# Two-layer trunk on one core: attention's output projection in products of 512 tokens, and a planner with another model of transfers

## The chip, the core and the metric

The kernel runs on one core of one Trainium2 chip. The metric is the device time of one execution in microseconds (us), the median of three runs; lower is better. The profiled execution is a run of its own, with its own time.

## The reference, cut to what matters

There are 1024 tokens of width 1024, fp32 throughout. Layer 0 mixes tokens with a sparse attention (an indexer scores all earlier keys, the best 256 are kept), layer 1 with a gated short convolution. Each mixer is followed by a SwiGLU network of hidden width 2816.

```python
for i in range(DEPTH):                       # DEPTH = 2
    mod = c_act @ ada_w[i] + ada_b[i]        # six vectors of 1024: shift, scale, gate, twice
    sh1, sc1, g1, sh2, sc2, g2 = [m[:, None, :] for m in jnp.split(mod, 6, axis=-1)]
    h = _rmsnorm(x, norm1_g[i]) * (1.0 + sc1) + sh1
    y = _dsa_mixer(h, ...) if i % 2 == 0 else _short_conv_mixer(h, ...)
    x = x + g1 * y
    h = _rmsnorm(x, norm2_g[i]) * (1.0 + sc2) + sh2
    x = x + g2 * _swiglu(h, w_gate, w_up, w_down)
# the end of _dsa_mixer: o is what attention gives, (1024 tokens, 1024)
    return o @ w_out                         # the product that the change is about
```

## The kernel before, in words

Every large product is made in three parts so that it keeps fp32's precision: each operand is split into a rounded half and the remainder, "hi" and "lo", and `mm3` issues hi*hi, hi*lo and lo*hi into the same PSUM bank. A weight comes from DRAM into a buffer `raw` (512 KB, two buffers) and is split by ScalarE (`whi`, a cast) and VectorE (`wlo`, a subtraction); some weights are first combined with others on VectorE (the tiles `s`).

The kernel's functions do not issue instructions in the order in which they are written. They record them in a planner, `Plan`, which then simulates the engines on the host: `cost` gives each instruction a duration, `drain` takes at each step the instruction that can start first (ties and preferences by a priority `pri`), and emits it. Each engine then runs its own list strictly in order. Because `drain` emits everything, nearly all instructions carry one line in the profile, L278. For a transfer the planner keeps one clock, `self.dma`, that advances by the bytes at a fixed rate, and takes the data as there some time after that clock. All of these transfers are issued from one queue, SyncE's (SP). Some copies (`plan.copy`) may go to ScalarE or VectorE, whichever the planner finds free sooner.

The program on TensorE runs through these stages, with times of the profiled execution: start-up (0 to 60 us), the input projection, the indexer and the selection (60 to 290), attention over eight blocks of 128 queries (290 to 591), the second half of the output projection (591 to 640), the first network (640 to about 1290), the convolution layer (about 1290 to 1580), and the second network (to 2261).

Attention's normalised output of one block of queries and one group of four heads is written by `group_end`: `tk.split` writes the hi and lo parts. Before, `attend` allocates for each pair of blocks (256 tokens) one tile `ohi` and one tile `olo` of [128, 8, 256], out of rings of three buffers. The tiles of blocks 6 and 7 so take the buffers of blocks 0 and 1.

The output projection works on halves of 512 tokens (blocks 0 to 3, blocks 4 to 7) and on eight column tiles d of 128 columns. `out_tile(half, d)` loads the weights' columns, takes a PSUM bank of 512 columns, fills its two halves of 256 columns from the two pairs (8 steps of k, three products each, so 48 products), and adds the gated result to the residual x with one VectorE instruction. Half 0 is spread over the attention blocks 4 and 5, one tile after each group of heads (380 to 492 us). Half 1 follows the last block, in `attended` (591 to 640 us); there the residual tiles are `xr` in the profile, in half 0 they are `x`.

A second kind of work is threaded through attention and later stages: the conditioning vectors. `ada_next` loads 256 KB of `ada_w` into `adaw` (two buffers) and adds it, scaled, to the sum `adacc` on VectorE. Such a step on VectorE waits for its load, and its load can only start when the step two before it has freed the buffer.

Of the kernel before, what the change touches and what calls it, by code (L numbers as in the profile page):

```python
# [10 lines left out]
F32R = mybir.dt.float32r  # L11
# [4 lines left out]
ALU = mybir.AluOpType  # L16
# [89 lines left out]

class Op:
    __slots__ = ("eng", "cost", "emit", "pri", "left", "ready", "users", "end", "stores", "lat",
                 "late", "other", "form", "table", "needs", "parked")

    def __init__(self, eng, cost, emit, pri, lat=0.0):
        self.eng, self.cost, self.emit, self.pri, self.lat = eng, cost, emit, pri, lat
# [73 lines left out]
class Plan:  # L186
# [6 lines left out]
    ROWS, COLS = (64, 128), (128, 64)  # L193
    CHANGE = {(ROWS, None): 0.285, (None, ROWS): 0.115, (None, COLS): 0.12, (COLS, None): 0.15,
              (ROWS, COLS): 0.277, (COLS, ROWS): 0.278}
    TRAIL = 1.0 / 450e3
    SPAN, SHAKE = 100, ()
    TABLES, SWITCH = (AF.Silu, AF.Sqrt, AF.Sin, AF.Exp), 1.28
    STAY = 4.0
# [37 lines left out]
    def cost(self, eng, fn, out, ins, kw):  # L237

        n = out.free
        if fn == "dma_start":  # L240
            if eng == "gpsimd":
                return 0.85, 1.6
            inside = len(ins) == 1 and all(r.store.alloc is not None for r in ins + [out])
            return {"sync": 0.65 if inside else 0.475, "scalar": 0.1}[eng], 1.6
        if eng == "tensor":
            if fn == "transpose":
                return 0.107, 0.0
            if ins[1].dtype in (F32R, BF16):
                return max(n, 64) * 17 / 38400.0, 0.0
            return max(n * 4, 512) / (4800.0 if HD in (ins[0].free, ins[0].shape[0]) else  # L250
                                      2400.0), 0.0
        psum = any(r.store.space == PSUM for r in ins + [out])
        m = max([n] + [r.free for r in ins])
        aps = sum(r.free == 1 for r in ins)
        if eng == "scalar":
            slow = {AF.Silu: 0.06, AF.Square: 0.03}.get(kw.get("func"), 0.0)
            return ((0.05 if (ins or [out])[0].store.space == PSUM else 0.095) + 0.84e-3 * n + slow +
                    (0.09 if "accum_out" in kw else 0.0) + 0.1 * aps), 0.0
        if eng == "vector":
            if fn == "memset":  # L260
                return 0.02 + 1.04e-3 * (n if n > P else 0), 0.0
            if fn in ("tensor_scalar", "tensor_copy") and not psum and "accum_out" not in kw:
                return 0.08 + (0.52e-3 if fn == "tensor_copy" else 0.59e-3) * m, 0.0
            if fn in ("tensor_tensor_scan", "reciprocal"):
                return 0.07 + (2.07e-3 if fn == "tensor_tensor_scan" else 6.25e-3) * m, 0.0
            if fn == "tensor_scalar" and "accum_out" in kw:
                return 0.14 + 1.04e-3 * m, 0.0
            return max(0.09, 0.078 + 1.04e-3 * m) + (0.05 * aps if m > 64 else 0.0), 0.0
        if fn in ("memset", "affine_select"):
            return 0.05 + 1.4e-3 * n, 0.0  # L270
        a, w = (0.28, 1.95e-3) if fn == "tensor_tensor" else (0.43, 1.3e-3)
        return a + w * (n - 1), 0.0
# [43 lines left out]
    def record(self, eng, fn, args, kw, other=None):  # L316
        vals = list(args) + list(kw.values())
        outs = [kw["out"] if "out" in kw else args[0]]
        if "accum_out" in kw:
            outs.append(kw["accum_out"])  # L320
        refs = [v for v in vals if isinstance(v, Ref)]
        ins = [v for v in refs if not any(v is o for o in outs)]
        emit = self.emitter(eng, fn, args, kw)
        shaped = outs[0] if isinstance(outs[0], Ref) else refs[0]
        func = {"func": args[2]} if fn == "activation" else {}
        cost, lat = self.cost(eng, fn, shaped, ins, {**kw, **func})
        op = Op(eng, cost, emit, self.rank(), lat)
        if "accum_out" in kw:
            op.late = 0.13 if eng == "vector" else 0.1
        if eng == "scalar" and fn == "activation":  # L330
            op.table = args[2] if args[2] in self.TABLES else None
        if other is not None:
            op.other = (other[0], self.cost(*other[:2], shaped, ins, kw)[0],
                        self.emitter(*other, args, kw))
        if fn == "dma_start":
            op.lat = lat + shaped.free * shaped.shape[0] * 4 / 380e3
        self.note(op, refs, outs)
        return op

# [157 lines left out]
    def drain(self, *pools):  # L497

        held = []
        while any(p.pending for p in pools) if pools else True:  # L500
            best, again = None, False
            for e in self.ENGINES:
# [3 lines left out]
                op = got[3][-1]  # L506
# [18 lines left out]
            t, e, heap, v = best  # L525
            op = v[-1]
# [11 lines left out]
                t = max(t, self.free[e] + self.SWITCH)  # L538
            self.free[e] = end = t + cost
            if op.lat:  # L540
                self.dma = max(self.dma, end) + (op.lat - 1.6)
                end = self.dma + 1.6 + (op.lat - 1.6) * 380e3 * self.TRAIL
                if e == "sync":
                    self.free[e] = max(self.free[e], self.dma - 2.5)
            for st in op.stores:
                if st.alloc is not None:
                    st.pool.pending -= 1
# [42 lines left out]
def blk(b):  # L590
    return slice(b * P, (b + 1) * P)
# [318 lines left out]
class Attention:  # L910
    ON_DVE, X_SECOND, X_WORK = 5, 24.5, 38.0
    T_PROJ, SLOT = 45.0, 6.2
    ON_ACT, IDX = (2, 3, 6, 7), 0.5

    def __init__(self, tk, w, w_out, ada_w, xspill):
        self.tk, self.nc, self.w, self.w_out = tk, tk.nc, w, w_out
# [419 lines left out]

    def attend(self):
        tk, nc, plan = self.tk, self.nc, self.plan
        self.o, self.banks, self.rows, tail = [], 0, 0, None
        self.steps = [(layer, j, i, k) for layer, j in ((0, 2), (0, 3), (0, 4), (0, 5), (1, 0))  # L1340
                      for i in range(NH) for k in range(KT)]
        for b in range(TB):
            if b % 2 == 0:
                self.o.append([self.op.tile([P, KT, 2 * P], F32R, name="o%s%d" % (v, b),
                                            tag="o" + v, bufs=3) for v in ("hi", "lo")])
            t0, t1 = self.t_att[b], self.t_att[b + 1]
            plan.pri = t0 - 12.0
            q = (self.at if b % 2 else self.keep).tile([P, T], F32, name="qst", tag="qst",
# [117 lines left out]
    def group_end(self, b, g, ops, sums):  # L1466
# [11 lines left out]
        flat = on.rearrange("p r t -> p (r t)")  # L1478
        plan.copy(flat, ops[:, 0:2 * P])
        nc.vector.tensor_tensor(flat, flat, bc, op=ALU.mult)  # L1480
        hi, lo = (v.part_of((b % 2, g))[:, 2 * g:2 * g + 2, blk(b % 2)] for v in self.o[b // 2])
        tk.split(on, hi, lo)

    def out_tile(self, half, d, keep=None):

        tk, nc = self.tk, self.nc
        w = tk.wcols(self.w_out, d * P, P)
        xt = self.at.tile([P, HW], F32, name="x1", tag="x1") if keep is None else keep
        nc.sync.dma_start(xt, self.xspill[half][d])
        ps = self.bank("out")  # L1490
        for i in range(2):
            ohi, olo = self.o[2 * half + i]
            for k in range(KT):
                tk.mm3(ps[:, i * 2 * P:(i + 1) * 2 * P], *w(k), ohi[:, k, :], olo[:, k, :],
                       k == 0, k == KT - 1)
        nc.vector.scalar_tensor_tensor(xt, ps, tk.mod[0][2][:, d:d + 1], xt,
                                       op0=ALU.mult, op1=ALU.add)
        if keep is None:
            nc.sync.dma_start(self.xspill[half][d], xt)

# [523 lines left out]
```

## Time and profile before

| quantity | value |
|---|---|
| median of three runs | 2261.14 us (2258.73 to 2264.98) |
| profiled execution, whole time | 2262.64 us |
| its span, first to last instruction | 2260.9 us |
| mean granted TensorE clock | 0.987 |
| TensorE busy | 2207.6 us of the span |
| VectorE busy | 1896.3 us |
| ScalarE busy | 1136.8 us |
| data moved by transfers | 353.74 MB |

PE is TensorE, PEld its weight loads, DVE VectorE, ACT ScalarE, SP SyncE (which here only issues transfers). A row of the chain of waits tells what the end of the program depended on, in order of time: start, length, what. A row of the windows view gives a stretch, its length, the busy time of PE, PEld, DVE, ACT and POOL in it with the number of instructions, the granted clock of TensorE, the share of the DMA engines and GB/s.

### The profile page before, as it was taken

The numbers are of one execution on the slowest core, as the hardware profiler recorded it, in microseconds if no ns is written. First come the engines' busy times: TensorE is split into PE (matmuls) and PEld (weight loads), VectorE is DVE, ScalarE is ACT, GpSimd is POOL, SyncE is SP. The second block draws the span as 40 slices with busy tenths as digits, with TensorE's granted clock in tenths as the row PEclk, the third lists the DMA queues.
The fourth block names the chain that finished last, engine by engine and source line by source line (L and its number), as shares of the span: only waits on it lengthen the run. The fifth ranks groups of instructions, "written<-read, shape, count | busy, mean of one in ns | idle before, by whom it ended". The sixth has DMA issues, their size and how long they took to land.

```text
span 2260.9 us, 32683 instructions
## 1 busy us (share of the span) xinstructions
PE 2207.6 (98%) x11499; PEld 1790.8 (79%) x11499; DVE 1896.3 (84%) x3819; ACT 1136.8 (50%) x2162; POOL 4.8 (0%) x19
## 2 busy tenths in 40 slices
PE   6999989999999999999999999999999999999999
PEld 5758856876888778888888787878888888888887
DVE  7899999798599989887798899886898877768974
ACT  5487999767664333333445552224553333334444
POOL 0000000000000000000000000000000000000000
PEclk7999989999999999999999999999999999999999
DMA  9413233543364656455982454234445432349824
GB/s 317 124 41 103 89 108 102 167 131 99 104 177 141 212 184 192 138 170 179 384 279 84 123 152 143 86 117 158 122 126 183 152 120 87 125 145 387 286 86 139
DMA packets 332318, 353.74 MB, mean 156 GB/s; under 512 B 19289, under 2 KB 216954, under 8 KB 332154
## 3 DMA queue, kind: packets, MB, share of 16 engines
q1 hardware_dynamic: 331944, 351.52, 48.8%
q8 instruction: 90, 1.47, 0.3%
q14 instruction: 74, 0.61, 0.1%
q10 hardware_dynamic: 210, 0.14, 0.0%
HBM read 278.97 MB, written 68.94 MB: 154 GB/s over the span
## 4 chain that ended last, share of the span: by engine, by line
PE 78%; DVE 13%; DMA 4%; issue 2%; ACT 2%; POOL 0%; ACTq 0%; SPq 0%; DVEq 0%; POOLq 0%
PE ps_g L278 44%; PE ps_mm L278 31%; DVE wlo L278 2%; PE ps_o L278 2%; DVE u L278 1%; DVE s L278 1%; PE ps_L L278 1%; DMA adaw<-in_ada_w_dram 1%; DVE sc L278 1%; DVE p L278 1%; DVE adacc L278 1%; DVE karena L278 1%; DMA raw<-in_conv_w_in_dram 1%; DMA ph<-in_ffn_w_down_dram 1%; DVE v L278 0%
## 5 line engine op out<-in xcount | busy, mean ns | idle before, releaser
L278 ACT CAST whi<-raw 128x512 fp32r<-128x512 f32 x307 | 189.4, 620 | 360.4 <-PE ps_g L278 150.0
L278 PE MATMUL ps_g<-t,whi 128*128 128x512 f32 x1184 | 366.1, 390 | 3.0 <-ACT whi L278 3.0
L278 ACT CAST whi<-s 128x512 fp32r<-128x512 f32 x276 | 171.1, 621 | 317.7 <-PE ps_g L278 133.7
L278 PE MATMUL ps_g<-h,whi 128*128 128x512 f32 x1056 | 327.6, 391 | 0.5 <-ACT whi L278 0.5
L278 DVE TENSOR_TENSOR wlo<-raw,whi 128x512 fp32r<-128x512 f32 x312 | 213.2, 687 | 74.4 <-ACT whi L278 74.0
L278 PEld LDWEIGHTS ps_g<-t,whi 128*128 128x128 f32 x1184 | 222.1, 188 | 50.1 <-ACT whi L278 4.3
L278 PE MATMUL ps_g<-t,wlo 128*128 128x512 f32 x592 | 231.1, 391 | 3.6 <-DVE wlo L278 3.4
L278 PEld LDWEIGHTS ps_g<-h,whi 128*128 128x128 f32 x1056 | 198.2, 188 | 42.1 <-ACT whi L278 1.4
L278 PE MATMUL ps_g<-h,wlo 128*128 128x512 f32 x528 | 206.3, 391 | 2.0 <-DVE wlo L278 2.0
L278 DVE TENSOR_TENSOR wlo<-s,whi 128x512 fp32r<-128x512 f32 x276 | 188.5, 686 | 18.3 <-ACT whi L278 17.7
L278 PE MATMUL ps_mm<-t,whi 128*128 128x512 f32 x608 | 189.3, 392 | 2.7 <-ACT whi L278 2.7
L278 PE MATMUL ps_g<-ph,whi 128*128 128x512 f32 x572 | 179.1, 389 | 0.0
L278 PEld LDWEIGHTS ps_mm<-t,whi 128*128 128x128 f32 x608 | 114.8, 189 | 27.9 <-ACT whi L278 3.6
L278 PEld LDWEIGHTS ps_g<-t,wlo 128*128 128x128 f32 x592 | 111.2, 188 | 29.6 <-DVE wlo L278 6.1
L278 PEld LDWEIGHTS ps_g<-ph,whi 128*128 128x128 f32 x572 | 107.3, 188 | 22.4
L278 PE MATMUL ps_mm<-t,wlo 128*128 128x512 f32 x304 | 119.7, 394 | 1.6 <-DVE wlo L278 1.6
L278 ACT ACTIVATE junk<-sc,bs 128x384 bf16<-128x384 f32 (+3 forms) x124 | 110.1, 888 | 16.0 <-DVE bs L278 9.7
L278 PEld LDWEIGHTS ps_g<-h,wlo 128*128 128x128 f32 x528 | 99.5, 189 | 23.3 <-DVE wlo L278 2.5
L278 DVE TENSOR_TENSOR u<-u 128x512 f32<-128x512 f32 x170 | 114.4, 685 | 1.9 <-ACT u L278 0.5
L278 DVE SCALAR_TENSOR_TENSOR adacc<-adaw,cact,adacc 128x512 f32<-128x512 f32 x140 | 104.4, 746 | 13.5 <-DMA adaw<-in_ada_w_dram 13.0
L278 PE MATMUL ps_g<-ph,wlo 128*128 128x512 f32 x286 | 110.3, 389 | 0.0
L278 PE MATMUL ps_mm<-ph,whi 128*128 128x512 f32 x308 | 96.6, 390 | 0.1
(328 smaller groups left out, 4792.8 us busy)
## 6 DMA issues: line engine op xcount, KB each, us to landing
adaw<-in_ada_w_dram SPq DMA_DIRECT2D x160, 256.0 KB, 3.2
ph<-in_ffn_w_down_dram SPq DMA_DIRECT2D x66, 512.0 KB, 6.7
raw<-in_ffn_w_gate_dram SPq DMA_DIRECT2D x54, 512.0 KB, 4.3
raw<-in_ffn_w_up_dram SPq DMA_DIRECT2D x54, 512.0 KB, 4.3
raw<-in_conv_w_in_dram SPq DMA_DIRECT2D x34, 512.0 KB, 5.1
raw<-in_ffn_w_down_dram SPq DMA_DIRECT2D x44, 256.0 KB, 2.6
ph<-in_ffn_w_down_dram SPq DMA_DIRECT2D x44, 256.0 KB, 4.7
raw<-in_attn_w_in_dram SPq DMA_DIRECT2D x18, 512.0 KB, 3.9
```

What stands on the lines that cost most here:

```text
L278: f(*[a.get() if isinstance(a, Ref) else a for a in args], **{k: a.get() if isinstance(a, Ref) else a for k, a in kw.items()})
```

## The change

It has two parts.

First, attention's output lies in one tile `ohi` and one `olo` of [128, 8, 3, 256], with three places for pairs of blocks; pairs 0, 1, 2, 3 take places 0, 1, 2, 1. `out_tile` issues 24 products of 512 columns for a column tile in place of 48 of 256: for half 0 from places 0 and 1, for half 1 from places 1 and 2. For half 1 the places stand in the other order than the tokens, so there the addition to the residual is made in two instructions of 256 columns.

Second, the planner's model: a product of n columns costs (n + 32) / 2400 us where it was n * 17 / 38400 (the same at 512 columns); a transfer's clock runs at 390 KB/us instead of 380, at 1.3 times the bytes where the last dimension is at most 128; the data is taken as there at the later of that clock plus 0.8 us plus a latency, and the issue plus the latency plus the bytes at 200 KB/us; the latency is 1.0 us, or 0.4 us for a transfer into DRAM, where it was 1.6. No instruction's work changes by this, only the order in which the lists are written (and which engine takes some copies).

```diff
@@ Plan: the planner's model @@
-    TRAIL = 1.0 / 450e3
+    RATE, ALONE, SHORT = 390e3, 200e3, 1.3
...
@@ cost @@
             if eng == "gpsimd":
-                return 0.85, 1.6
+                return 0.85, 1.0
             inside = len(ins) == 1 and all(r.store.alloc is not None for r in ins + [out])
-            return {"sync": 0.65 if inside else 0.475, "scalar": 0.1}[eng], 1.6
+            return {"sync": 0.65 if inside else 0.475, "scalar": 0.1}[eng], 1.0
...
             if ins[1].dtype in (F32R, BF16):
-                return max(n, 64) * 17 / 38400.0, 0.0
+                return (max(n, 64) + 32) / 2400.0, 0.0
...
@@ record @@
         if fn == "dma_start":
-            op.lat = lat + shaped.free * shaped.shape[0] * 4 / 380e3
+            op.bytes = shaped.free * shaped.shape[0] * 4 * (self.SHORT if shaped.shape[-1] <= P else 1)
+            inside = isinstance(outs[0], Ref) and outs[0].store.alloc is not None
+            op.lat = lat if inside else lat - 0.6
...
@@ drain @@
             if op.lat:
-                self.dma = max(self.dma, end) + (op.lat - 1.6)
-                end = self.dma + 1.6 + (op.lat - 1.6) * 380e3 * self.TRAIL
+                self.dma = max(self.dma, end) + op.bytes / self.RATE
                 if e == "sync":
                     self.free[e] = max(self.free[e], self.dma - 2.5)
+                end = max(self.dma + 0.8 + op.lat, end + op.lat + op.bytes / self.ALONE)
...
@@ the attention class, attend @@
+    PLACES = (0, 1, 2, 1)
...
+        self.o = [self.op.tile([P, KT, 3, 2 * P], F32R, name="o" + v) for v in ("hi", "lo")]
...
         for b in range(TB):
-            if b % 2 == 0:
-                self.o.append([self.op.tile([P, KT, 2 * P], F32R, name="o%s%d" % (v, b),
-                                            tag="o" + v, bufs=3) for v in ("hi", "lo")])
...
@@ group_end @@
-        hi, lo = (v.part_of((b % 2, g))[:, 2 * g:2 * g + 2, blk(b % 2)] for v in self.o[b // 2])
+        i = self.PLACES[b // 2]
+        hi, lo = (v.part_of((i, b % 2, g))[:, 2 * g:2 * g + 2, i, blk(b % 2)] for v in self.o)
         tk.split(on, hi, lo)
...
@@ out_tile @@
         ps = self.bank("out")
-        for i in range(2):
-            ohi, olo = self.o[2 * half + i]
-            for k in range(KT):
-                tk.mm3(ps[:, i * 2 * P:(i + 1) * 2 * P], *w(k), ohi[:, k, :], olo[:, k, :],
-                       k == 0, k == KT - 1)
-        nc.vector.scalar_tensor_tensor(xt, ps, tk.mod[0][2][:, d:d + 1], xt,
-                                       op0=ALU.mult, op1=ALU.add)
+        places = self.PLACES[2 * half:2 * half + 2]
+        i = min(places)
+        for k in range(KT):
+            keys = [(p, r, k // 2) for p in places for r in range(2)]
+            tk.mm3(ps, *w(k), *(v.part_of(keys)[:, k, i:i + 2].rearrange("p i t -> p (i t)")
+                                for v in self.o), k == 0, k == KT - 1)
+        gate = tk.mod[0][2][:, d:d + 1]
+        for c in ((0, HW),) if places[0] == i else ((2 * P, HW), (0, 2 * P)):
+            j = 0 if c[0] == 0 and c[1] == HW else 2 * P - c[0]
+            x = xt[:, j:j + c[1] - c[0]]
+            nc.vector.scalar_tensor_tensor(x, ps[:, c[0]:c[1]], gate, x, op0=ALU.mult,
+                                           op1=ALU.add)
```

The second part, with the new durations of the first, moves instructions on all engines. Three places follow; names before the arrow are written, names behind it read.

TensorE, end of attention, before: the output projection's half 1 has begun, in the gap ahead of the last products with the values, `ps_o` (`ohi_3024` and `olo_3025` belong to blocks 4 and 5; `whi` and `wlo` are weights).

```order
L278 MATMUL ps_mm<-ohi_3024,wlo 128x256
L278 MATMUL ps_mm<-ohi_3024,whi 128x256
L278 MATMUL ps_mm<-olo_3025,whi 128x256
L278 MATMUL ps_o<-pf,vst 64x128 x16
L278 MATMUL ps_mm<-ohi_3024,wlo 128x256
L278 MATMUL ps_mm<-ohi_3024,whi 128x256
L278 MATMUL ps_mm<-olo_3025,whi 128x256
```

The same place after:

```order
L278 MATMUL ps_mm<-ohi,whi 128x512
L278 MATMUL ps_mm<-olo,whi 128x512
L278 MATMUL ps_mm<-ohi,wlo 128x512
L278 MATMUL ps_o<-pf,vst 64x128 x16
L278 MATMUL ps_mm<-ohi,whi 128x512
L278 MATMUL ps_mm<-olo,whi 128x512
L278 MATMUL ps_mm<-ohi,wlo 128x512
```

Ahead of `ps_o` stand six products of 512 columns now, where eleven of 256 did; behind it the projection goes on, now with pieces of blocks 6 and 7 in every product.

VectorE, in the first network (about 789 to 800 us), before: steps of the conditioning (`adacc`), the network's gating (`u`, `v`, `cv`) and weights in preparation (`s`, `wlo`).

```order
L278 SCALAR_TENSOR_TENSOR adacc<-adaw,cact,adacc 128x512
L278 TENSOR_TENSOR wlo<-s,whi 128x512
L278 TENSOR_TENSOR u<-cv,ps_mm 128x512
L278 TENSOR_TENSOR v<-u 128x512
L278 TENSOR_TENSOR cv<-cv 128x512
L278 TENSOR_TENSOR v<-v,ps_g 128x512
L278 SCALAR_TENSOR_TENSOR adacc<-adaw,cact,adacc 128x512
L278 TENSOR_TENSOR u<-u,ps_g 128x512
L278 SCALAR_TENSOR_TENSOR adacc<-adaw,cact,adacc 128x512
L278 TENSOR_TENSOR u<-u 128x512
L278 TENSOR_TENSOR wlo<-raw,whi 128x512
L278 TENSOR_TENSOR u<-u,ps_g 128x512
```

The same place after:

```order
L278 SCALAR_TENSOR_TENSOR adacc<-adaw,cact,adacc 128x512
L278 TENSOR_TENSOR wlo<-s,whi 128x512
L278 TENSOR_TENSOR cv<-cv 128x512
L278 TENSOR_TENSOR u<-cv,ps_mm 128x512
L278 TENSOR_TENSOR v<-u 128x512
L278 SCALAR_TENSOR_TENSOR adacc<-adaw,cact,adacc 128x512
L278 TENSOR_TENSOR v<-v,ps_g 128x512
L278 TENSOR_TENSOR s<-raw 128x512 x2
L278 SCALAR_TENSOR_TENSOR adacc<-adaw,cact,adacc 128x512
L278 TENSOR_TENSOR u<-u,ps_g 128x512
L278 TENSOR_TENSOR wlo<-raw,whi 128x512
L278 TENSOR_TENSOR u<-u 128x512
```

The second `adacc` of these rows moved ahead by two instructions, and two `s<-raw` moved from behind the third `adacc` to ahead of it.

SyncE's transfers at the beginning of the convolution layer (from about 1284 us), before: weights (`raw`), conditioning (`adaw`), and a spilled tile `cv` (written to `aw`, read back later).

```order
L278 DMA adaw<-in_ada_w_dram 128x512
L278 DMA raw<-in_conv_w_in_dram 128x8x128 x2
L278 DMA adaw<-in_ada_w_dram 128x512
L278 DMA aw_0_184<-cv 128x512
L278 DMA adaw<-in_ada_w_dram 128x512
L278 DMA aw_1_185<-cv 128x512
L278 DMA raw<-in_conv_w_in_dram 128x8x128
L278 DMA adaw<-in_ada_w_dram 128x512 x2
L278 DMA aw_0_186<-cv 128x512
L278 DMA aw_1_187<-cv 128x512
L278 DMA raw<-in_conv_w_in_dram 128x8x128
```

After, the next loads of `adaw` stand further on, among the reads of the spilled tiles:

```order
L278 DMA adaw<-in_ada_w_dram 128x512
L278 DMA cv<-aw_0_184 128x512
L278 DMA raw<-in_conv_w_in_dram 128x8x128 x2
L278 DMA cv<-aw_1_185 128x512
L278 DMA adaw<-in_ada_w_dram 128x512
L278 DMA hid_0_91<-cv 128x512
L278 DMA cv<-aw_0_186 128x512
L278 DMA adaw<-in_ada_w_dram 128x512
L278 DMA cv<-aw_1_187 128x512
L278 DMA cv<-aw_0_188 128x512
L278 DMA raw<-in_conv_w_in_dram 128x8x128 x2
L278 DMA cv<-aw_1_189 128x512
```

The five loads of `adaw` that stood among the first writes of `cv` moved about 70 us of the program further, to among the reads.

More of the change, by code (lines that the diff above doesn't have):

```diff
@@ L108 @@
     __slots__ = ("eng", "cost", "emit", "pri", "left", "ready", "users", "end", "stores", "lat",
-                 "late", "other", "form", "table", "needs", "parked")
+                 "late", "other", "form", "table", "bytes", "needs", "parked")
     def __init__(self, eng, cost, emit, pri, lat=0.0):
@@ L1338, in attend @@
         tk, nc, plan = self.tk, self.nc, self.plan
-        self.o, self.banks, self.rows, tail = [], 0, 0, None
+        self.banks, self.rows, tail = 0, 0, None
+        self.o = [self.op.tile([P, KT, 3, 2 * P], F32R, name="o" + v) for v in ("hi", "lo")]
         self.steps = [(layer, j, i, k) for layer, j in ((0, 2), (0, 3), (0, 4), (0, 5), (1, 0))
```

## The prediction

> **What bounds the kernel now.** I read the page's busy times and its summary of the chain first, then the windows view cut at the stages, then the chain and the waits inside the stretches that the change touches.
>
> ```profile
> span 2260.9 us, 32683 instructions
> PE 2207.6 (98%) x11499; PEld 1790.8 (79%) x11499; DVE 1896.3 (84%) x3819; ACT 1136.8 (50%) x2162; POOL 4.8 (0%) x19
> PE 78%; DVE 13%; DMA 4%; issue 2%; ACT 2%; POOL 0%; ACTq 0%; SPq 0%; DVEq 0%; POOLq 0%
> ```
>
> PE is busy for 2207.6 of 2260.9 us and carries 78% of the chain; 53.3 us are left in which it does nothing. The windows say where those are.
>
> ```profile
> 0.00:60.00 60.00, 40.39 (x203) 35.51 (x204) 43.80 (x93) 32.73 (x57) 1.76 (x13) 0.74 0.92 321
> 290.00:380.00 90.00, 82.98 (x658) 52.82 (x656) 88.08 (x335) 88.32 (x248) 0.00 (x0) 0.92 0.34 95
> 380.00:492.00 112.00, 109.53 (x1006) 92.45 (x1005) 93.96 (x285) 80.74 (x167) 0.00 (x0) 1.00 0.49 144
> 591.00:640.00 49.00, 49.00 (x426) 48.70 (x425) 35.64 (x60) 25.61 (x43) 0.00 (x0) 1.00 0.52 164
> 640.00:780.00 140.00, 139.96 (x627) 115.72 (x626) 130.24 (x218) 65.51 (x110) 0.00 (x0) 1.00 0.59 180
> 780.00:810.00 30.00, 24.45 (x92) 18.32 (x91) 24.21 (x41) 8.66 (x15) 0.00 (x0) 0.89 0.64 201
> 810.00:1280.00 470.00, 469.45 (x2085) 387.33 (x2084) 400.62 (x651) 194.13 (x332) 0.00 (x0) 1.00 0.58 193
> 1280.00:1300.00 20.00, 17.95 (x77) 14.37 (x76) 17.85 (x35) 8.49 (x15) 0.00 (x0) 0.91 0.60 180
> 1300.00:1360.00 60.00, 60.00 (x265) 49.22 (x264) 59.94 (x101) 33.86 (x59) 0.00 (x0) 1.00 0.54 156
> 1360.00:1400.00 40.00, 36.09 (x155) 28.02 (x154) 37.96 (x68) 9.49 (x16) 0.00 (x0) 1.00 0.46 136
> 1400.00:1580.00 180.00, 177.46 (x777) 145.03 (x777) 146.02 (x247) 57.62 (x98) 0.00 (x0) 1.00 0.40 121
> ```
>
> The reader is to see three kinds of stretch. In 591 to 640 (half 1 of the output projection), 640 to 780 and 810 to 1280 PE has no gap: only less PE work makes these shorter, and another order of the other engines gains nothing there. In 290 to 380, 1300 to 1360 and 1360 to 1400 DVE (88.08 of 90, 59.94 of 60, 37.96 of 40) is about as full as PE. And in 780 to 810 and 1280 to 1300 neither is full: PE lacks 5.55 and 2.05 us and its granted clock falls to 0.89 and 0.91, worth another 0.11 x 30 = 3.3 and 0.09 x 20 = 1.8 us. An order of work can win or lose in the last two kinds and at start-up (19.6 us of idle PE beside a DMA share of 0.92).
>
> **The change, part by part. The products.** Half 1 on the chain of waits, and a run of 512-column products from the stage behind it:
>
> ```profile
> 594.60 15.55 PE ps_mm L278 x128
> 615.70 24.35 PE ps_mm L278 x203
> 657.73 2.72 PE ps_mm L278 x12
> ```
>
> A product of 256 columns follows the one before after 24.35 / 203 = 0.120 us (15.55 / 128 = 0.1215 agrees); one of 512 takes 2.72 / 12 = 0.2267 us. Two of the former become one of the latter: 0.240 - 0.2267 = 0.0133 us saved per pair. There are 8 tiles x 8 steps x 3 products x 2 pairs = 384 products in a half before and 192 after, so 192 x 0.0133 = 2.56 us a half.
>
> In half 1 the whole of it is on the path, since PE is busy 49.00 of 49.00 us: -2.56. Nothing else becomes late there: DVE has 35.64 us of work and ACT 25.61 in what will be 46.4 us. The bounds are the same row's two ends, 15.55 / 128 and 24.35 / 203: -2.56 to -2.85.
>
> In half 0 the products lie between attention's groups, in eight pieces of 48 x 0.120 = 5.76 us that become 5.44. PE is busy 109.53 of 112 us there, so it is the bound nearly throughout, but 2.47 us of waits show that DVE and ACT are close behind at some groups. All of it saved gives -2.56; none saved (each group then waits for its softmax instead) gives 0. I take -2.0, nearer to the first since PE's idle share is only 2%.
>
> One rule speaks against this price. The Trainium skill, "TensorE: Matmul & The Clock Gate", section "Back-to-back issue gap", gives an isolated product's spacing as N / 2.4 + 2.5 ns. By it a pair of 256 columns would take 218.3 ns and one of 512 takes 215.8, so all 384 pairs would save an estimated 1.0 us and not 5.1. The trace does not agree: it has 120 ns and 226.7 ns, a fixed part of about 13 ns for each product; the rows decide the sum.
>
> **The split addition.** In half 1 eight additions of 512 columns become sixteen of 256.
>
> ```profile
> L278 DVE SCALAR_TENSOR_TENSOR xr<-ps_mm,mod,xr 128x512 f32<-128x512 f32 x7 | 5.2, 748 | 0.8 <-PE ps_mm L278 0.8
> L278 DVE TENSOR_TENSOR on<-on,ps_mm 128x256 f32<-128x256 f32 x1 | 0.4, 421 | 6.4 <-ACT on L278 6.4
> ```
>
> Two of 421 ns for one of 748: 0.094 us x 8 = +0.75 us of DVE, which has 13 us to spare in the stage. What follows the last of them on PE is the first network, and 640 to 780 shows PE without a gap across that border, so the cover is the products of 512 tokens already normalised. I take 0; without the cover the last tile alone would be late, by 0.1 us, and at most by all 0.75.
>
> **The dependency that could have appeared** is that place 1 is written a second time, by blocks 6 and 7. They wait for half 0's products, as they did for the ring of three. Half 0 ends at about 492 us, and the first group of block 6 is written after that in either order: 0. At the end of attention six products of 512 (6 x 0.2267 = 1.36 us) stand ahead of the last `ps_o` where eleven of 256 (1.32 us) did, so the gap there stays filled: 0. The products behind it need blocks 6 and 7 only as far as they are done, and 18 products are free of the last group: 4.1 us, against a first visit to those blocks 3.6 us after the start (30 x 0.120) before. Bounds 0 to +1.
>
> **The new order: the conditioning in attention.** An `adacc` step waits on DVE until its load is there, and the load starts when the step two before has freed the buffer.
>
> ```profile
> DVE adacc L278 <- DMA adaw<-in_ada_w_dram: 6.8, 8, 1.2
> adaw<-in_ada_w_dram SPq DMA_DIRECT2D x160, 256.0 KB, 3.2
> ```
>
> In 380 to 492 DVE waited so 8 times, 6.8 us in all. A load takes 3.2 us from issue to landing. I counted, in the order of DVE and with the durations of the trace, the steps of attention that have less than 3.2 us of other DVE work since the buffer became free: 17 of 78 before, 22 after; the missing work sums to 10 us before and 16 after. So waits grow by 5 x (6.8 / 17) = +2.0 us on DVE, at most by the 6 us that are missing more. PE's idle time there is 2.47 us beside those 6.8, so about a third passes on: +0.7 (0 to +2.2). Behind the waiting step stand the maxima of the next group's scores, which ACT's exponentials and then PE wait for.
>
> **The stall in the first network.**
>
> ```profile
> 790.28 7.09 DMA adaw<-in_ada_w_dram
> DVE adacc L278 <- DMA adaw<-in_ada_w_dram: 3.3, 2, 2.2
> ACT whi L278 <- DVE s L278: 10.7, 5, 7.1
> 799.47 4.63 PE ps_mm L278 x10
> ```
>
> In 780 to 810 a load of `adaw` is issued at 790.28 us and lands 7.09 us later. DVE waits for it and its predecessor, 3.3 us in all; the weights `s` stand behind on DVE and ACT waits up to 7.1 us for them, and then PE. When PE starts again, ten products take 4.63 us, 0.463 each and so twice 0.2267: the clock has halved. The change moves two `s<-raw` (0.6 us each) ahead of the second wait, into time that DVE idles, so the weights behind are 1.2 us earlier; `wlo<-raw`, which PE needs first, still stands behind the same load. I take -1.2 (-4 if the load lands early enough to spare the clock's drop of 3.3 as well, +3 if one more load is caught so, the size of the 3.3 us of waits now).
>
> **The convolution layer.** Five `adaw` loads, and their steps, move from 1284 to 1300 into 1350 to 1400. There DVE has 97.9 of 100 us of work from 1300 on.
>
> ```profile
> ACT whi L278 <- DMA raw<-in_conv_w_in_dram: 14.2, 3, 5.3
> 1385.34 5.45 DMA raw<-in_conv_w_in_dram
> ```
>
> Five steps are 5 x 0.68 = 3.4 us of DVE that come out of a stretch with 2.15 us of DVE slack and go into one without, but DVE arrives there that much earlier. The loads of `raw` (one takes 5.45 us on the chain) also stand up to two places earlier in SP's queue, though they still wait for DVE to free their buffer. I take 0, between -3.9 (all of the idle PE time of 1360 to 1400) and +3.4.
>
> At start-up the weights' first loads and the transposes swap places; nothing shows which way it goes: 0, with 2 us to either side, about a tenth of its idle PE time of 19.6.
>
> **The sum.** -2.56 - 2.0 + 0 + 0.7 - 1.2 + 0 + 0 = -5.06 us, against the profiled span of 2260.9: 2255.8, and a whole time of 2262.64 - 5.06 = 2257.6. That execution stands 1.5 us above the median of 2261.14, so the median should come to 2256.1. All runs before lie between 2258.73 and 2264.98, so 0.3% (6.8 us: 2254.4 and 2267.9) is about what can be told from no change, and the forecast lies within it.
>
> **Rivals.**
> Faster, by the order: the planner's new view of transfers takes away most of what transfers cost now. For it speaks that 780 to 810, 1280 to 1300 and 1360 to 1400 hold 8.85 + 3.85 + 3.9 = 16.6 us of idle or slow PE, each with a load on the chain. Against it: in the last of these DVE is full, and in the first the same load still stands ahead. If half of it goes, 8.3 instead of my 1.2, the time is 2256.1 - 7.1 = 2249.0.
>
> Slower: the five conditioning steps in the convolution layer wait for their loads. DVE is the bound there, so each wait goes to the end in full; a load's 3.2 us five times is 16 us, and the time is 2256.1 + 16 = 2272. It would be slower than no change by over 0.3% from 11.8 us on, 2.4 us a step. For it speaks the stall at 790.28, which is this mechanism in the stage before; against it, that in attention 17 close steps cost only 6.8 us, 0.4 each. The Trainium skill, "TensorE: Matmul & The Clock Gate", section "Why this matters for your kernels", warns that a gap of TensorE over about 3 us brings half speed back; the ten products at 799.47 agree.
>
> No gain: half 0 saves nothing, because its groups wait for the softmax, and the waits for `adaw` grow by the full 2.2: -2.56 + 2.2 = -0.4, so 2260.8.
>
> **How the numbers follow.** Likeliest case 0.50, at 2256.1 with about 4 us to either side (2252 to 2260) from the terms at 780 to 810, the convolution and the start-up taken together; 0.14 of this lies below 2254.4, the rest within 0.3%. The faster rival 0.26, all but 0.01 below 2254.4. No gain 0.10, within. The slower rival 0.14, of which 0.01 ends within. Faster 0.14 + 0.25 = 0.39, same 0.36 + 0.01 + 0.10 + 0.01 = 0.48, slower 0.13. The range takes in the faster rival with 3 us below it (2246) and ends above at 2266, where the slower case has half its waits (2256.1 + 8 = 2264); what lies outside is some 0.12 above and 0.06 below.
>
> **What would show it.** Products on the chain at 0.2267 us in both halves, and half 1 about 46.4 us long with PE full; if it is still 49, the first term is wrong. In blocks 4 and 5 PE's idle time should be 2.5 to 4 us; over 5 means that half 0's saving went into waits for the softmax. The waits of `adacc` for `adaw` in attention should grow by about 2 us. Around 790 to 800 us an `adacc` should still wait, with half-speed products behind it; without them the faster rival is right. In 1360 to 1400 the list of waits should have no `adacc` over 1 us; several of 2 to 3 us are the slower rival. All stages that PE fills now should keep their length within 0.5 us. The prediction fails most easily by an order of work that leaves a stage of the second network, now without gaps, with a new one.

## The result, and the profile after

The changed kernel takes 2274.28 us (2265.66 to 2276.12, 12 runs) where the kernel before takes 2260.96 (2258.73 to 2264.98, 12 runs): a ratio of 1.0055, interval 1.0047 to 1.0062. It is 13.3 us slower; 2256.1 was forecast, and the range ended at 2266.

The page of the changed kernel, its span, its busy times and its summary of the chain:

```profile
span 2273.4 us, 32007 instructions
PE 2215.1 (97%) x11115; PEld 1777.2 (78%) x11115; DVE 1899.9 (84%) x3832; ACT 1130.3 (50%) x2157; POOL 4.9 (0%) x19
PE 73%; DVE 14%; DMA 6%; issue 3%; ACT 3%; SPq 0%; ACTq 0%; POOL 0%; DVEq 0%; POOLq 0%
```

PE has 384 products fewer and is busy 7.5 us longer. The view of the cores has the reason, the mean granted clock:

```profile
core 0: 2273.4 us, clock 0.982
```

It was 0.987. That is 0.018 x 2273.4 = 40.9 us of lost clock where it was 0.013 x 2260.9 = 29.4, so about +11.5 us; idle PE grew from 53.3 to 2273.4 - 2215.1 = 58.3, +5.0; the products should give back 5.1. These add up to +11.4 of the span's +12.5. It is a balance and not yet a cause: some 3 us of the lost clock lie in the first 60 us (0.69 where it was 0.74), and the table below shows no lag there.

The windows of the changed kernel, cut as before:

```profile
0.00:60.00 60.00, 41.89 (x204) 37.04 (x205) 42.42 (x92) 31.98 (x55) 1.77 (x13) 0.69 0.94 325
60.00:290.00 230.00, 223.47 (x1150) 171.57 (x1149) 210.47 (x597) 169.97 (x367) 3.18 (x6) 0.98 0.27 81
380.00:492.00 112.00, 108.42 (x813) 80.67 (x812) 98.06 (x301) 79.78 (x167) 0.00 (x0) 0.98 0.50 151
591.00:640.00 49.00, 48.92 (x333) 40.80 (x332) 30.34 (x58) 29.64 (x53) 0.00 (x0) 1.00 0.44 140
780.00:810.00 30.00, 24.87 (x98) 18.25 (x97) 26.13 (x45) 6.22 (x12) 0.00 (x0) 0.93 0.73 228
1280.00:1300.00 20.00, 20.00 (x90) 16.57 (x89) 19.55 (x32) 14.57 (x26) 0.00 (x0) 1.00 0.34 107
1360.00:1400.00 40.00, 37.82 (x158) 30.16 (x157) 39.61 (x70) 9.22 (x15) 0.00 (x0) 0.96 0.47 145
```

Before, the second of these rows read:

```profile
60.00:290.00 230.00, 226.58 (x1211) 175.04 (x1211) 213.49 (x614) 174.11 (x378) 3.00 (x6) 1.00 0.30 88
```

The clock is lower at start-up and in stretches that had 1.00 before (60 to 290, 380 to 492, 1360 to 1400). Since everything shifts, windows at fixed times mix stages. So I took the start of the same product in both traces and subtracted; what the table has is the median over 10 us of the changed kernel's lag, by the time that the product had before.

| time before, us | 65 | 85 | 250 | 375 | 405 | 585 | 645 | 1250 | 1310 | 1420 | 1510 | 1610 | 2050 | 2200 |
|---|---|---|---|---|---|---|---|---|---|---|---|---|---|---|
| lag of the changed kernel, us | -0.2 | 6.4 | 7.2 | 8.6 | 12.2 | 10.7 | 8.3 | 9.5 | 5.4 | 3.9 | 8.2 | 9.8 | 9.8 | 12.7 |

Seven of the thirteen microseconds appear between 65 and 85 us, long before attention's output exists; 3.6 at about 390, 4.3 at about 1480, 2.9 at about 2130, against gains of 2.4 in half 1 and of 5.6 from 1250 to 1420.

**The place at 65 to 85 us.** TensorE's rows in order of time, of the changed kernel; in brackets the idle time ahead and what ended it:

```profile
69.37 0.45 PE L278 MATMUL ps_mm<-hlo,kwhi 128*72 128x512 f32 x1 [0.80 <-DVE hlo L278]
70.64 0.39 PE L278 MATMUL ps_mm<-hhi,wlo 128*128 128x256 f32 x1 [0.59 <-DVE wlo L278]
72.91 0.71 PE L278 MATMUL ps_o<-ident,s 72*128 72x72 f32 x4 [0.78 <-DVE sc L278]
```

The same stretch before, with its one wait:

```profile
69.45 0.50 PE L278 MATMUL ps_mm<-hhi,whi 128*128 128x512 f32 x1 [0.32 <-ACT s L278]
```

Windows of 3.4 us over it, changed kernel:

```profile
68.40:71.80 3.40, 2.01 (x14) 1.36 (x13) 3.40 (x8) 0.58 (x1) 0.00 (x0) 1.00 0.07 19
71.80:75.20 3.40, 2.62 (x15) 2.28 (x13) 2.40 (x7) 0.00 (x0) 0.00 (x0) 0.50 0.19 49
75.20:78.60 3.40, 3.40 (x24) 3.19 (x23) 2.65 (x4) 0.00 (x0) 0.00 (x0) 0.50 0.76 233
78.60:82.00 3.40, 3.40 (x18) 3.40 (x17) 2.28 (x9) 0.58 (x2) 0.00 (x0) 0.50 0.26 85
82.00:85.40 3.40, 3.40 (x20) 2.95 (x19) 1.94 (x5) 0.37 (x1) 0.00 (x0) 1.00 0.02 5
```

After a window in which PE was busy for 2.01 of 3.40 us the clock (third from the right) is 0.50 for three windows, though PE is busy throughout the last two. Two of the three waits, 0.80 and 0.59 us, lie in that window; the third, 0.78, comes when the clock has fallen. DVE is full at 3.40 of 3.40 in the window ahead of the fall, and PE waits for its `hlo`, then for its `wlo`. DVE's rows there, of the changed kernel:

```profile
67.90 0.75 DVE L278 TENSOR_TENSOR rt<-rt,C 128x256 f32<-128x256 f32 x2
68.57 0.74 DVE L278 SCALAR_TENSOR_TENSOR hlo<-nz,mod,hhi 128x512 fp32r<-128x512 f32 x1
69.24 0.75 DVE L278 TENSOR_TENSOR rt<-rt,sw 128x256 f32<-128x256 f32 x2
69.91 2.49 DVE L278 TENSOR_TENSOR wlo<-raw,whi 128x512 fp32r<-128x512 f32 x4
```

The same rows before:

```profile
67.16 0.74 DVE L278 SCALAR_TENSOR_TENSOR hlo<-nz,mod,hhi 128x512 fp32r<-128x512 f32 x1
67.82 0.76 DVE L278 TENSOR_TENSOR rt<-rt,C 128x256 f32<-128x256 f32 x2
68.49 0.76 DVE L278 TENSOR_TENSOR rt<-rt,sw 128x256 f32<-128x256 f32 x2
69.16 2.50 DVE L278 TENSOR_TENSOR wlo<-raw,whi 128x512 fp32r<-128x512 f32 x4
```

The last `hlo` starts 1.4 us later: DVE as a whole is 0.7 us late, and two rotary products (`rt`, 0.7 us) stand ahead of it now. That is the new order at work; the kernel's arithmetic is the same.

### The profile page after: what moved, and what is told of

It reads as the page before. It is cut to its first block, busy times and chain, and to the rows that moved or that the text cites. A ratio compares the mean times of both kernels' runs of the same rounds, so it can differ in the third digit from the quotient of the medians.

```text
span 2273.4 us, 32007 instructions
## 1 busy us (share of the span) xinstructions
PE 2215.1 (97%) x11115; PEld 1777.2 (78%) x11115; DVE 1899.9 (84%) x3832; ACT 1130.3 (50%) x2157; POOL 4.9 (0%) x19
## 4 chain that ended last, share of the span: by engine, by line
PE 73%; DVE 14%; DMA 6%; issue 3%; ACT 3%; SPq 0%; ACTq 0%; POOL 0%; DVEq 0%; POOLq 0%
PE ps_g L278 41%; PE ps_mm L278 28%; DMA ph<-in_ffn_w_down_dram 4%; PE ps_o L278 2%; PE ps_L L278 2%; DVE wlo L278 2%; DVE u L278 2%; DVE s L278 1%; DVE sc L278 1%; ACT junk L278 1%; DMA adaw<-in_ada_w_dram 1%; DVE ph L278 1%; DVE adacc L278 1%; DVE karena L278 1%; DVE xr L278 1%
## 5 line engine op out<-in xcount | busy, mean ns | idle before, releaser
L278 ACT ACTIVATE junk<-sc,bs 128x896 bf16<-128x896 f32 (+3 forms) x124 | 109.7, 885 | 20.0 <-DVE bs L278 11.9
L278 DVE SCALAR_TENSOR_TENSOR adacc<-adaw,cact,adacc 128x512 f32<-128x512 f32 x140 | 104.4, 746 | 12.9 <-DMA adaw<-in_ada_w_dram 12.5
L278 ACT CAST whi<-ph 128x512 fp32r<-128x512 f32 x66 | 41.1, 622 | 121.7 <-DVE ph L278 70.2
```

What stands on the lines that cost most here:

```text
L278: f(*[a.get() if isinstance(a, Ref) else a for a in args], **{k: a.get() if isinstance(a, Ref) else a for k, a in kw.items()})
```

## The experiments

The changed kernel has two parts that can be told apart. A planner's model that is put back writes the old lists again: up to attention, the kernel with the products alone has the lists of before row by row, and the one with the new model alone those of the changed kernel. Each ratio below is to runs of the kernel before on the same chip, in the same session (their medians are 2260.3 to 2261.7).

**The products alone** (e1): of the diff only the tile, `PLACES`, `group_end` and `out_tile`.

> The first part of the change alone: one tile with three places and products of 512, the planner's model as before. Its lists are those of before up to attention. Theory A (the new model's order costs the time, first of all by TensorE gaps at start-up that bring half clock at 72 to 82 us): 2256 to 2259, faster than before by 2 to 5 us, half clock nowhere from 55 to 290 us. Theory B (longer products hold attention's groups up): slower than before by 4 us or more, 2265 to 2270, with the lag growing at 380 to 492 us.

2256.04 us, ratio 0.998 (0.9971 to 0.999): 4.7 us faster, and there is no half clock from 55 to 290 us. The planner orders the longer products anew, so from 380 us on the lists of all engines differ from those of before in this kernel too. **The new model alone** (e2): the diff's other lines, with products of 256 and the ring.

> The second part alone: the new model of products and transfers, products of 256 and the ring of three tiles as before. Its lists are those of the changed kernel up to attention. Theory A: slower than before by 12 to 18 us, 2273 to 2279, half clock for 10 us at about 72 us. Theory B: within 3 us of before.

2273.04, ratio 1.0057 (1.0045 to 1.007). So the products gain and the model loses, as theory A has it; theory B falls. In e2's profile the start-up lags by 5.4 us at 250, though PE is not at half clock at 72 us but once, at 190.

**Only the start-up's order** (e3, e4): in `drain` and for a product's cost

```diff
-            if op.lat:
+            if op.lat and t < 75.0:      # e3: the old rule; e4 has t >= 75.0
+                ...the old rule
+            elif op.lat:
```

> The whole change, but the planner uses its old model up to 75 us of its own time, so that the start-up is ordered as before and the rest by the new model. Theory A: 6 to 8 us less than the changed kernel, 2266 to 2268, without half clock at 72 to 82 us. A rival C (the time goes in the stages from attention on, and the lag at start-up would be caught up there): within 3 us of the changed kernel, 2271 to 2277.

> The whole change, but the planner uses the new model only up to 75 us of its own time and the old one behind: the start-up is that of the changed kernel. Theory A: 6 to 8 us more than the kernel with the products alone, with half clock at 72 to 82 us, so 2262 to 2267. Rival C: as the products alone.

e3: 2261.16, ratio 1.0005 (0.9996 to 1.0014), 13 us less than the changed kernel where 6 to 8 were expected. e4: 2262.08, ratio 1.001 (1.0001 to 1.0019), 6.0 above the products alone, as expected, but without half clock at 72 to 82 us in its profile: against the products alone its lag is 3.4 us at 250, and another 3 come at about 400 to 440, with 3.4 us at half clock. So the start-up matters in both, and rival C falls. It also sets the order of what is planned behind it: behind 100 us, e3's list on VectorE differs from the changed kernel's in some 900 of 3700 rows, and e3 took back far more than the start-up's share. What is left of e3 against the products alone is 5.1 us, from orders behind the start-up.

**The half clock by itself** (e5): products with a tile of zeros into the waits, emitted behind the instruction that precedes the wait.

```diff
+        for _ in range(n):               # 4 of 512 columns, 5 and 6 of 256
+            self.plan.nc.tensor.matmul(out.get(), self.zero[:, 0:ins[0].shape[-1]].get(), ins[1].get(),
+                                        start=False, stop=False)
```

> The changed kernel with fifteen more products on TensorE, each by a tile of zeros, so that they add nothing: 4 of 512 columns and 11 of 256 at about 68 to 72 us, where the changed kernel's TensorE waited three times (0.80, 0.59 and 0.78 us) ahead of 10 us at half clock. Nothing else moves. Theory A1 (the short waits bring the half clock, and that costs time of its own): no half clock between 60 and 290 us, and 3 to 5 us less than the changed kernel, 2269 to 2272. Theory A2 (the clock only goes with waits that set the time anyhow): within 1.5 us of the changed kernel.

2272.24, ratio 1.0045 (1.0032 to 1.0057). Windows of e5 over the place:

```profile
66.50:69.90 3.40, 3.40 (x19) 2.28 (x17) 3.40 (x10) 1.20 (x2) 0.00 (x0) 1.00 0.00 0
69.90:73.30 3.40, 3.23 (x29) 2.97 (x29) 2.74 (x7) 0.12 (x1) 0.00 (x0) 1.00 0.19 48
73.30:76.70 3.40, 3.40 (x36) 3.22 (x35) 3.30 (x7) 0.37 (x1) 0.00 (x0) 1.00 0.45 111
```

PE is kept busy, the clock stays at 1.00, and the same products start 4.6 us earlier than in the changed kernel's first profile. At 189 us one window at half clock gives 1.6 back, so e5's profile ends 2.9 us earlier. Its median is 2.0 below 2274.28 and 5.2 below the changed kernel's in the same session (e8), but the intervals of these ratios overlap, so a gain at the end is not shown. Nor does one profile show that the filling kept the clock, as theory A1 has it: the clock's windows begin 2 us earlier in it (66.4 us in place of 68.4), and three profiles below kept the clock at this place with the waits unfilled.

**The changed kernel again** (e8):

> The changed kernel once more, for a second profile. If the half clock depends on where the clock's windows of 3.4 us fall against the short waits, the stretch at 72 to 82 us need not be slow in it, and the slow stretches lie at other places than in the first profile, with the times spread over 8 us or more; if the waits alone decide it, it is slow in the same places. Median as before, 2273 to 2275.

2277.47 (2271.51 to 2278.47), ratio 1.0061 (1.0047 to 1.0074), above the 2273 to 2275 that were expected. The stretch at 71 to 82 us is at half clock again. But e12 below, whose lists are those of the changed kernel up to the end of attention, has full clock there, with a window as empty:

```profile
67.60:71.00 3.40, 2.02 (x11) 1.13 (x10) 3.40 (x9) 1.01 (x2) 0.00 (x0) 1.00 0.01 4
71.00:74.40 3.40, 2.53 (x25) 2.22 (x24) 2.74 (x7) 0.00 (x0) 0.00 (x0) 1.00 0.21 54
```

So have e2 and e4, whose lists are the changed kernel's up to about 390 and 270 us. First e2, then e4:

```profile
67.60:71.00 3.40, 2.02 (x10) 0.99 (x8) 3.40 (x10) 1.29 (x2) 0.00 (x0) 1.00 0.00 0
71.00:74.40 3.40, 2.54 (x22) 2.36 (x23) 2.74 (x7) 0.02 (x1) 0.00 (x0) 1.00 0.19 48
```

```profile
67.40:70.80 3.40, 2.00 (x11) 1.14 (x10) 3.40 (x8) 0.97 (x2) 0.00 (x0) 1.00 0.03 7
70.80:74.20 3.40, 2.53 (x25) 2.22 (x24) 2.74 (x7) 0.00 (x0) 0.00 (x0) 1.00 0.20 51
```

These are five profiles of one and the same start-up list:

| run | start of the clock's window with the first waits, us | half clock behind it | lag at 85 us | lag at 250 us |
|---|---|---|---|---|
| changed kernel | 68.4 | 10.2 us | 6.4 | 7.2 |
| e8 | 68.0 | 10.2 us | 6.1 | 6.9 |
| e12 | 67.6 | none | 2.4 | 3.2 |
| e2 | 67.6 | none | 2.8 | 5.4 (half clock at 190) |
| e4 | 67.4 | none | 2.1 | 3.0 |

So of the start-up's 7 us some 3 are the order's and some 4 the half clock that it risks. The two with half clock are those whose windows begin latest; no run sets where the windows begin, so it is not shown that this decides.

**Which rule of the model** (e6, e7, e9 to e12, e17, e18). e6 is the products with the new cost of a product and the old transfer rules, e7 the reverse; the others change these constants or lines of the changed kernel (lines cut at `...`):

```
 e9  -RATE, ALONE, SHORT = 390e3, 200e3, 1.3    +..., SHORT = 1.0
 e10 -RATE = 390e3                              +RATE = 380e3
 e11 -end = max(self.dma + 0.8 + op.lat, ...)   +end = self.dma + op.lat + 0.6 + op.bytes / 450e3
 e12 -ALONE = 200e3                             +ALONE = 900e3
 e17 RATE = 380e3, SHORT = 1.0
 e18 SHORT = 1.0                                +end = self.dma + 1.6 + op.bytes / 450e3
```

The old rule has 1.6 us for every transfer. So has e18; in e11 a transfer into DRAM is taken as done after 1.0, so its landing is not wholly the old one.

> The products of 512 with the old model of transfers and the new cost of a product, (n + 32) / 2400. Theory D (no rule of the model is bad; any new order is a draw, and the old one was a good draw): anywhere from 2256 to 2274, by gaps and half clock in other places than in the changed kernel. Theory E (the transfer rules alone do the harm): as the products alone, 2254 to 2258.

> The products of 512 with the new model of transfers and the old cost of a product. Its start-up is that of the changed kernel but for a few instructions. Theory D: 3 to 6 us above the products alone from the start-up, the rest a draw: 2259 to 2276. Theory E: as the changed kernel, 2272 to 2276.

> The changed kernel without the factor 1.3 for transfers with a last dimension up to 128 (SHORT = 1). Theory F (one rule of the transfer model does the harm): if it is this rule, 2256 to 2260, else 2271 to 2277. Theory G (the orders differ by chance, each change of the model is a new draw): somewhere between, 2259 to 2271.

> The changed kernel with the transfers' clock at 380 KB/us as before in place of 390, all else as changed. It is a change of 2.6% of one constant. Theory F: 2271 to 2277, since so small a step can't be the rule that matters. Theory G: it moves over a thousand instructions of VectorE's list, and the time moves with them, by 4 us or more to either side of 2274.

> The changed kernel with the old rule for when data is there (the transfers' clock plus 1.6 us plus the bytes at 450 KB/us) and the new clock (390 KB/us and the factor 1.3). Theory F: if the earlier landing is the harmful rule (VectorE and ScalarE then get steps ahead of their data), 2256 to 2260, else 2271 to 2277. Theory G: between.

> The changed kernel without the lower bound by a lone transfer's rate (ALONE at 900 KB/us in place of 200). Its start-up is that of the changed kernel to the instruction, the rest differs in some 400 rows of VectorE. Theory F: 2256 to 2260 if it is this rule, else 2271 to 2277. Theory G: the start-up keeps its 3.5 to 7 us, the rest is a new draw: 2262 to 2276.

> Products of 512 and the new cost of a product; of the transfer rules the new landing alone (latency 1.0 or 0.4, the later of two bounds), with the clock at 380 KB/us and no factor 1.3. Theory H (the harm is in the clock's rate and the factor): 2256 to 2260. Theory I (the landing does harm of its own, in that it takes data as there about 1 us sooner): 2264 to 2275.

> Products of 512 and the new cost of a product; of the transfer rules the rate of 390 KB/us alone, with the old landing and no factor 1.3. Theory H: if the rate is the harmful part, 2264 or more; if it is the factor 1.3, 2256 to 2260. Theory I: 2256 to 2260.

| transfers' clock in the model | old landing | new landing |
|---|---|---|
| 380, no factor | e6: 2257.8 (0.9973 to 0.999) | e17: 2258.4 (0.9984 to 1.0002) |
| 380, factor 1.3 | not run | e10: 2261.7 (0.9994 to 1.0012) |
| 390, no factor | e18: 2263.9 (1.0004 to 1.0022) | e9: 2265.0 (1.0009 to 1.0027) |
| 390, factor 1.3 | e11: 2275.7 (1.0055 to 1.008) | changed kernel: 2274.3 (1.0047 to 1.0062) |

The intervals are of the ratio to before. e7 (the old cost of a product, else as changed) took 2274.8 (1.0045 to 1.007), and e12 2263.6 (0.9999 to 1.0017). So the new cost of a product is harmless (e6, theory E on that point; E's 2272 to 2276 holds for e7 too, though both lie in theory D's wide ranges as well), and so is the new landing alone (e17, theory H, which e18 misses by 0.1; theory I falls). The rate costs 6 us alone, the factor 3 (e10 and e17, whose intervals overlap, so this is not clear of noise), and both 16 to 18 together. Theory G has e9, e10 and e12 in its ranges and misses e11. Theory F, one rule, falls: three edits, of the rate, of the factor and of the lone transfer's bound, take back 9 to 13 us each.

**Is it the model or a draw?** (e13 to e16): the old model's rate at 376 and 384 KB/us, the new one's at 386 and 394.

> The products of 512 with the old model, its one rate at 376 KB/us in place of 380. Theory G1 (the order is a draw whichever the model; that of the products alone was a lucky one): its lists move as far as they do between the models (some 800 rows of VectorE), so 2258 to 2272. Theory G2 (the old model's orders are better as such): 2254 to 2259, as with 380.

> The products of 512 with the old model, its one rate at 384 KB/us. VectorE's start-up stays as with 380. Theory G1: 2256 to 2270; theory G2: 2254 to 2259.

> The changed kernel with the transfers' clock at 386 KB/us in place of 390. Theory G1: 2258 to 2272, as the old model's draws, most likely below the changed kernel, which was an unlucky draw. Theory G2: 2268 to 2277.

> The changed kernel with the transfers' clock at 394 KB/us in place of 390. Theory G1: 2258 to 2272. Theory G2: 2268 to 2277.

2259.67 (0.9985 to 1.0003) and 2256.24 (0.997 to 0.9988); 2269.79 (1.0023 to 1.0047) and 2268.84 (1.0022 to 1.0048). The old model's orders lie at 2256 to 2260, the new model's at 2262 to 2274. A step of the rate moves the time by up to 8 us, and either way (new model at 380, 386, 390, 394: 2261.7, 2269.8, 2274.3, 2268.8), which is the draw. The two sets do not overlap, which speaks for the model; but they are three orders against four, and the intervals of the two nearest, e13 and e10 (0.9994 to 1.0012), overlap. Theory G1's ranges are wide and hold all four of these runs; of G2's, e13 is 0.7 above the bound, and the new model at 380 (e10) lies below the 2268 it gave. So that the new model's orders are worse as such fits these runs best and is not shown. No run shows why orders by the faster clock and the factor are worse. In 20 to 40 us, with the transfers full, 370 GB/s were moved before and 374 in the changed kernel, so the old rate of 380 was nearer there than 390 (which the factor 1.3 lowers again for short rows); whether that is the reason was not tried.

## Why the prediction was wrong, step by step

**The products, half 1: right.** Predicted -2.56. The lag falls from 10.7 to 8.3, -2.4; with the products alone it goes from +0.1 at 585 to -2.3 at 645, the same. The chain of waits of the products alone (e1) in the stage:

```profile
594.75 14.51 PE ps_mm L278 x63
614.72 23.40 PE ps_mm L278 x103
```

23.40 / 103 = 0.227 us a product, as taken. PE stays full there (49.00 of 49 in e1). The bound of -2.85 was a slip: 15.55 / 128 gives 192 x (0.2430 - 0.2267) = -3.1. The figure that follows from the Trainium skill ("TensorE: Matmul & The Clock Gate", section "Back-to-back issue gap"), 2.5 ns saved a pair and not 13.3, does not hold here.

**Half 0: near the right size, but given back behind it.** Predicted -2.0. With the products alone the lag goes from -0.3 at 375 to -1.7 at 500, where half 0 has ended: -1.4. In the changed kernel it falls from 12.2 at 405 to 10.0 at 500, and PE's idle time of 112 - 108.42 = 3.6 us is within the 2.5 to 4 that were named as the sign. But at 585 the products alone are back at +0.1, so blocks 6 and 7 lose 1.8 (in the changed kernel 0.7). The sum had nothing for that, and no run shows its cause. That e1 came out at the forecast 2256 all the same is luck: its order gained in the convolution layer, where in its profile the lag goes from -3.4 at 1250 to -8.5 at 1510. (That profile ends 8.6 us ahead of the one before, where the medians are 4.7 apart, so a usual run gains less.)

**The split addition: right on the path, its size off.** Changed kernel, by shape:

```profile
L278 DVE SCALAR_TENSOR_TENSOR xr<-ps_mm,mod,xr 128x256 f32<-128x256 f32 x12 | 5.7, 478 | 1.9 <-PE ps_mm L278 1.9
```

Two of 478 ns for one of 748 are +1.7 us of DVE in eight tiles, not +0.75; PE's lag does not show it.

**The conditioning in attention: the waits grew as forecast, the passing on was wrong.** In 290 to 591 us DVE's waits for `adaw`, before and then changed:

```profile
DVE adacc L278 <- DMA adaw<-in_ada_w_dram: 7.8, 10, 1.2
```

```profile
DVE adacc L278 <- DMA adaw<-in_ada_w_dram: 9.0, 12, 1.7
```

That is +1.2 us where +2.0 was predicted. (In 380 to 492 alone, from where the price was taken, they fell from 6.8 to 4.0 us.) But a third was to reach the end, and one wait alone cost 3.6 us, the half clock that followed it included. The changed kernel's chain there:

```profile
380.17 4.84 DMA adaw<-in_ada_w_dram
385.10 0.75 DVE adacc L278
...
386.21 1.13 ACT junk L278 x2
...
389.31 1.54 PE ps_mm L278 x6
```

A load of 4.84 us holds `adacc`, behind it stand a selection's scalars on DVE and the pass `junk` on ACT, and PE, kept waiting, is at half clock from 389.2 to 392.6 us. The average rate of passing on left that out.

**The stall in the first network: mis-sized.** Predicted -1.2; the lag is 8.3 at 770 and 8.3 at 830. Half clock came in two windows of it again. Behind it, in a stretch that PE fills and that was to keep its length within 0.5 us, the lag rises from 8.1 at 1100 to 9.5 at 1180; that was not traced further.

**The convolution layer: 0 was right in sum**, +0.3 from 1250 to 1610, out of -5.6 up to 1420 and +4.3 at about 1480, where the changed kernel's chain has ten products at half clock again:

```profile
1484.52 4.14 PE ps_g L278 x10
```

The slower rival was not what happened: no `adacc` waits for `adaw` at all in 1300 to 1500. Its 2272 lies near the measured time by luck.

**The start-up: the step that failed.** It stood at 0 with 2 us to either side, "about a tenth of its idle PE time", a bound that came from no row. It is +7.2 in the changed kernel's first profile: some 3 us of waits for a DVE that has fallen behind, and some 4 of half clock behind them. By medians, the new start-up alone (e4) costs 6.0. The first profile's lag at the end is 12.7 where -5.06 was forecast; of these 17.8 us the start-up has 7.2, the stages from 250 to 585 4.8 (+3.5 where -2.0 + 0.7 stood), the first network 2.4, the second 2.9 and the rest 0.5. All of it but the products comes of the new order, of which the sum priced only the few places that were looked at. The rows that would have told are those of 60 to 75 us, in which DVE is full and PE runs without a margin; I looked for idle time to win or lose in stretches that had it, and had written that others can only be touched in their products. A stretch with none can lose its cover.

**The second network: named as the easiest way to fail, not priced.** Its lag grows by 2.9 at about 2130. The waits there for the weights of the last product, before and then changed, in 2090 to 2160 us:

```profile
DVE ph L278 <- DMA ph<-in_ffn_w_down_dram: 4.2, 3, 1.5
```

```profile
DVE ph L278 <- DMA ph<-in_ffn_w_down_dram: 7.5, 8, 1.7
```

The faster rival, by which the new view of transfers takes away stalls, got its 1280 to 1300 (PE is 20.00 of 20 at clock 1.00 there, the lag falls by 4.1) and gave back more elsewhere.

## What to carry to other kernels

A change of a scheduler's costs is a new order everywhere, and must be priced as such: build it alone and the code's part alone, since here one gained 4.7 us and the other lost 12.3. A full engine is no protection against a new order; where TensorE has no gap, count what the engine ahead of it has in hand. The products alone, with the planner's model as it was, are the best version that was run (2256.04; 2256.24 with the rate at 384).

## What the runs showed of the hardware

TensorE's clock halved at 71.8 us in the changed kernel, after a window of 3.4 us with two waits of 0.80 and 0.59 us; no single one was near 3 us. The Trainium skill, "TensorE: Matmul & The Clock Gate", section "Why this matters for your kernels", warns of gaps over about 3 us, and this trace differs: a window of 3.4 us that is busy for 2.01 us was enough here, and one busy for 2.02 us (e12) was not. The ten half-speed products of the kernel before, at 799.47 us, which the prediction took as agreeing, also had a shorter gap ahead of them, 2.69 us (794.8 to 797.5). Nor does PE's busy time in a window decide it: in e5 half clock followed one with 3.00 of 3.40 us (185.9 to 189.3), and in the changed kernel full clock followed one with 1.73 (187.9 to 191.3). What does decide stays open. The Trainium skill, same title, section "What's actually happening", has the clock set by a free-running window of 3413 ns; the trace agrees, with a stretch of 10.24 us (71.8 to 82.0), three such windows, and one of 3.4 (389.2 to 392.6). With one and the same list of instructions the half clock fell in two profiles of five, and where it fell it cost about 4 us at that place.
